# A hybrid decoder layer on one core: split weights of two column blocks kept in DRAM for the second row tile, row sums handed out over more units, first convolution product on ScalarE

## The chip, the cores and the metric

The kernel runs on one core of one Trainium2 chip. The metric is the device time of one execution in microseconds (us); lower is better. A core has a matrix engine (PE, with its weight loads listed as PEld), three engines for elementwise work (VectorE or DVE, ScalarE or ACT, GpSimd or POOL), a queue from which nearly all DMAs are issued (SP), and 16 DMA engines that carry them. Engines run their own instruction lists in a fixed order and wait for each other by semaphores.

## The reference, cut to what matters

One decoder layer on 2048 rows of width 1024. The attention half (two head groups, output projection, LayerNorm) is left as it is by the change. The change lies in the feed-forward half:

```
h = x * (1.0 + scale_f) + shift_f
gate = h @ w_ff_gate                 # 1024 x 2816
up   = h @ w_ff_up                   # 1024 x 2816
gp = jnp.pad(gate, ((0, 0), (CONV_WIDTH - 1, 0), (0, 0)))
conv = sum(gp[:, i:i + S, :] * conv_w[i] for i in range(CONV_WIDTH)) + conv_b   # width 3, along the rows
y = (jax.nn.silu(conv) * up) @ w_down
x = LayerNorm(alpha * x + (1 + gate_f) * y)
```

## The kernel before, in words

**Number format.** Every product is made of float32 operands split into a rounded part and a rest (`hi`, `lo`); three matmuls (hi by hi, hi by lo, lo by hi) stand for one. Splitting one weight part of 128 x 1024 costs a cast on ScalarE (`act.copy`) and a subtraction on VectorE or GpSimd (`tensor_sub`), both in `split`. These go through a helper that raises their priority; all that goes through it carries line 102 in the profile.

**The ring.** Split weights live in a ring of four pairs of tiles `w_hi`, `w_lo` (`ring_pair`). A pair is handed out in the order of the program text and comes free when everything that reads it is done. Raw weights land in `w_raw`, three buffers of 512 KB. In `weights` one part is one DMA into `w_raw`, one cast and one subtraction. For the attention projections `w_in_cols` already keeps the split parts: the first use splits and also stores both halves to DRAM, later uses load the halves into ring pairs.

**Rows and columns of the feed-forward half.** The 2048 rows are four tiles of 512 (0 to 3), taken as two pairs `t2` = 0 and 1. The 2816 columns are 11 blocks `fp` of 256. Most of the gate and up products are done by a seven-product scheme on a pair of row tiles: `unit(n)` is one block, gate or up, for a pair, with products numbered 0 to 6 (lines 1041 to 1043 in `product`). Its weights are made in four ring pieces c, a, b, d by `Weights.make`, and `need` makes pieces three ahead of the product that asks (`WAHEAD = 3`). Pieces c and d are split by ScalarE and VectorE; pieces a and b are sums on VectorE, then cast by ScalarE and subtracted by GpSimd.

**Plain products.** For row pair 0 the first two column blocks (`CL = 2`) are not done by units but by `plain(t, x)`, tile by tile: `plain(0, ...)` while the last tile of the attention half is still being finished, `plain(1, ...)` after the units of pair 0. One call handles two blocks; each block has two weight parts for gate and two for up, so 8 parts a call. Each part feeds 24 matmuls of 128x128 by 128x512 (`col_tile`, lines 293 to 295): 12 for each of the two 128-column halves. Gate sums stand in PSUM tiles `z`, up sums in `wt`, two buffers each.

**Order around the second seam.** Units 0 to 17 are pair 0 (`first` = 18). Unit 17's last call of `need` has by then made pieces c, a and b of unit 18 in the ring, ahead of the parts of `plain(1, ...)` in the program text. Then:

```
run(cols_todo)
spread(sets_of(1, (0, 1, 3, 4, 6)), 5, 5.0, plain(1, [b0[0], tsets[0, 5]]), 10.3 * 2 * CL)
run(sets_of(1, (2, 5)))
```

`sets_of` loads and splits the row operands `t` of pair 1 (DMAs `t<-dh`, `t<-dsum`). Operand sets 2 and 5 of pair 1 take the place of the ones that `plain(1, ...)` reads. `cols_todo` is 26 steps: 18 that transpose and modulate row tiles 2 and 3, then 8 that make sums of their operands on GpSimd (`store_sums`). It is taken three steps at a time after each unit from unit 3 on.

**Convolution.** `conv_silu` is three VectorE operations (lines 1143, 1144, 1145) and one ScalarE activation (line 1146): 40 times on 128x1024 in the units and 8 times on 128x512 in the plain products. Its input `gt` is written by VectorE and ScalarE, its output `cv` has two buffers, freed when their DMAs out (`dsa<-cv`, `da<-cv`) have landed.

Of the kernel before, what the change touches and what calls it, by code (L numbers as in the profile page):

```python
# [20 lines left out]
F32 = mybir.dt.float32  # L21
# [8 lines left out]
P = 128  # L30
# [3 lines left out]
KT = D // P  # L34
# [52 lines left out]
def layer(tc, x, c, w_ada, b_ada, w_in, gla_w_gate, gla_b_gate, sb_norm_g, gla_norm_g, w_out,  # L87
          ln1_g, ln1_b, w_ff_gate, w_ff_up, conv_w, conv_b, w_down, ln2_g, ln2_b, out):
    nc = tc.nc
# [15 lines left out]
    act, dve, pool = Urgent(nc.scalar), Urgent(nc.vector), Urgent(nc.gpsimd)  # L105
# [3 lines left out]
    w_ada, w_in, w_out = w_ada[0], w_in[0], w_out[0]  # L109
    w_ff_gate, w_ff_up, w_down = w_ff_gate[0], w_ff_up[0], w_down[0]  # L110
# [5 lines left out]
    dram = ctx.enter_context(tc.tile_pool(name="dram", bufs=1, space=DRAM))  # L116
# [15 lines left out]
    ccols = const.tile([P, 4 * NFF], F32, name="ccols")  # L132
# [15 lines left out]
    def ring_pair():  # L148

        pool, size = ext.get("pool"), ext.get("size", 0)  # L150
        i = ext.get("i", 0)
        ext["i"] = (i + 1) % (4 + size)
        if i < 4:
            return [wring.tile([P, 1024], F32R, name=f"w_{n}", bufs=4) for n in ("hi", "lo")]
        return [pool.tile([P, 1024], F32R, name=f"w_{n}x", bufs=size) for n in ("hi", "lo")]

    def split(raw, n, nw, lo_eng):
        hi, lo = (w[:, 0:1024 // nw * nw].rearrange("p (k c) -> p k c", c=nw) for w in ring_pair())
        act.copy(hi[:, 0:n], raw[:, 0:n])
        lo_eng.tensor_sub(lo[:, 0:n], raw[:, 0:n], hi[:, 0:n])  # L160
        return hi, lo

    def weights(src, lo_eng, nk=KT, scale=None):

        nw = src.shape[-1]
        per = 1024 // nw
        parts = []
        for k0 in range(0, nk, per):
            n = min(per, nk - k0)
            raw = wring.tile([P, 1024], F32, name="w_raw", bufs=3)  # L170
            raw = raw[:, 0:per * nw].rearrange("p (k c) -> p k c", c=nw)
            nc.sync.dma_start(raw[:, 0:n], src[k0 * P:(k0 + n) * P, :].rearrange("(k p) c -> p k c", p=P))
            if scale is not None:
                pool.tensor_mul(raw[:, 0:n], raw[:, 0:n], scale.unsqueeze(1).to_broadcast([P, n, nw]))
            parts.append(split(raw, n, nw, lo_eng))
        return parts

    dwi = {}

    def w_in_cols(c0, n, k0=0, nk=KT):  # L180

        key = c0, k0
        if key not in dwi:
            parts = weights(w_in[k0 * P:(k0 + nk) * P, c0:c0 + n], pool, nk)
            dwi[key] = []
            per = 1024 // n
            for i, hl in enumerate(parts):
                m = min(per, nk - i * per)
                kept = [dram.tile([P, m, n], F32, name=f"dwi{c0}_{k0}_{i}{j}") for j in "hl"]
                for w, d in zip(hl, kept):  # L190
                    nc.sync.dma_start(d, w[:, 0:m].bitcast(F32))
                dwi[key].append(kept)
            return parts
        parts = []
        for kept in dwi[key]:
            m = kept[0].shape[1]
            hl = [w[:, 0:1024 // n * n].rearrange("p (k c) -> p k c", c=n) for w in ring_pair()]
            for w, d in zip(hl, kept):
                nc.sync.dma_start(w[:, 0:m].bitcast(F32), d)
            parts.append(hl)  # L200
        return parts

    def load_x(t):
        xt = []
        for tb in range(NB):
            xx = pj.tile([P, D], F32, name="t4k", bufs=4)
            nc.sync.dma_start(xx, x[t * TQ + tb * P:t * TQ + (tb + 1) * P, :])
            xt.append(xx)
        return xt

    with tc.tile_pool(name="ada", bufs=1, reuse_waits="tile") as ada:
# [46 lines left out]
        if WLATE:  # L258
            for w, c0 in zip(w_first, (C_SBQ, C_SBK)):
                w += w_in_cols(c0, 256, 4, 4)  # L260
# [28 lines left out]
    def col_tile(ps, w, half, xh, xl, nk=KT, k0=0, k1=None):  # L289
        cs = slice(half * P, (half + 1) * P)  # L290
        for k in range(k0, k1 or nk):
            hi, lo = w[k // 4]
            nc.tensor.matmul(ps, hi[:, k % 4, cs], xh[k], start=(k == 0), stop=False)  # L293
            nc.tensor.matmul(ps, hi[:, k % 4, cs], xl[k], start=False, stop=False)  # L294
            nc.tensor.matmul(ps, lo[:, k % 4, cs], xh[k], start=False, stop=(k == nk - 1))  # L295
# [673 lines left out]
    def direct(i, src):  # L969

        out = []
        for k in range(4):
            w = t_tile(i, k)
            nc.sync.dma_start(w[:, 1, :].bitcast(F32), src[k])
            split_set(w, k)
            out.append(w)
        return out
# [162 lines left out]
    def conv_silu(cv, gt, fb):  # L1140

        n = cv.shape[-1]
        nc.vector.tensor_scalar_mul(cv, gt[:, 0:n], ccols[:, fb:fb + 1])
        nc.vector.scalar_tensor_tensor(cv, gt[:, 1:n + 1], ccols[:, NFF + fb:NFF + fb + 1], cv, ALU.mult, ALU.add)
        nc.vector.scalar_tensor_tensor(cv, gt[:, 2:n + 2], ccols[:, 2 * NFF + fb:2 * NFF + fb + 1], cv, ALU.mult, ALU.add)
        nc.scalar.activation(cv, cv, AF.Silu, bias=ccols[:, 3 * NFF + fb:3 * NFF + fb + 1])

    def plain(t, x):

        xh, xl = ([w[:, i, :] for half in x for w in half] for i in range(2))  # L1150
        for fp in range(CL):
            wg, wu = (weights(w[:, 256 * fp:256 * (fp + 1)], dve) for w in (w_ff_gate, w_ff_up))
            for j in range(2):
                fb = 2 * fp + j
                gp = psm.tile([P, TQ], F32, name="z")
                col_tile(gp, wg, j, xh, xl)
                gt, cv = (x[:, i * (TQ + 2):][:, 0:TQ + 2 - 2 * i] for x in [ft.tile([P, WIDTH["pl"]], F32, name="pl", bufs=2)]
                          for i in range(2))
                nc.gpsimd.tensor_copy(gt[:, 0:2], halo[:, fb, :])
                nc.scalar.copy(gt[:, 2:], gp)  # L1160
                nc.gpsimd.tensor_copy(halo[:, fb, :], gt[:, TQ:])
                conv_silu(cv, gt, fb)
                up = psm.tile([P, TQ], F32, name="wt")
                col_tile(up, wu, j, xh, xl)
                nc.vector.tensor_mul(cv, cv, up)
                nc.sync.dma_start(da[t // 2][:, t % 2 * NB:(t % 2 + 1) * NB, j, fp], cv.rearrange("p (b c) -> p b c", c=P))
                yield 10.3
# [18 lines left out]
    for n in range(first):  # L1186
        unit(n, (0, 2, 1, 3, 4, 5, 6) if n == 0 else range(7),
             {2: lambda: b0.append(direct(2, dh[1][0:4]))} if n + 1 == first else {})
        if n >= 3:
            for _ in range(3):  # L1190
                next(cols_todo, None)
    run(cols_todo)
    spread(sets_of(1, (0, 1, 3, 4, 6)), 5, 5.0, plain(1, [b0[0], tsets[0, 5]]), 10.3 * 2 * CL)
# [105 lines left out]
    for s, (i, b) in enumerate(steps):  # L1299
# [4 lines left out]
        for k in range(NH):  # L1304
            w = wset[i][k]
# [58 lines left out]
```

## Time and profile before

| | us |
|---|---|
| median of 3 runs | 2909.52 |
| lowest, highest | 2899.4, 2913.5 |
| the profiled execution, its own time | 2910.72 |
| its span, first to last instruction | 2909.0 |
| TensorE busy | 2695.8 (93%) |
| VectorE busy | 2092.0 (72%) |
| ScalarE busy | 1126.2 (39%) |
| GpSimd busy | 1206.8 (41%) |
| mean granted TensorE clock | 0.955 of full speed |

The page of the profile gives busy times and the span in 40 slices. The views of the trace used below are tables of stretches (busy time of each engine, granted clock, share of the DMA engines), lists of who waited for whom, groups of instructions by line and shape, and timelines of one engine. In a timeline, a bracket gives the idle time before the instruction and what ended it. A stretch's time is counted from the start of the span. The attention half ends at about 1570 us; units of pair 0 fill the stretch from there to about 1985, `plain(1, ...)` stands between about 1985 and 2047, units of pair 1 follow to about 2480, then comes the down projection.

### The profile page before, as it was taken

Reading aid. Unit: us, or ns where it says so; the run is one execution under the profiler, and the core shown is the slowest. Engines: PE = TensorE matmul, PEld = TensorE weight load, DVE = VectorE, ACT = ScalarE, POOL = GpSimd, SP = SyncE. Lnnn points to the kernel's source line nnn. Section 1 sums busy time; section 2 is a strip of 40 time slices with the busy share of each in tenths; the row PEclk is TensorE's granted clock in tenths of the full one; section 3 lists DMA queues with packets and bytes.
Section 4 is the critical chain, followed back from the end, with each engine's and each line's share of the span. In section 5 each row is a group of like instructions: output and inputs, shape, how many; then the busy total and the mean of one; then the engine's idle time right before and its main releaser. Section 6 shows DMA issues by size and latency. Waiting matters only on the chain. (4 is left out here: it accounts for less than half of the span.)

```text
span 2909.0 us, 38667 instructions
## 1 busy us (share of the span) xinstructions
PE 2695.8 (93%) x13123; PEld 2176.0 (75%) x13123; DVE 2092.0 (72%) x2984; ACT 1126.2 (39%) x1955; POOL 1206.8 (41%) x1271
## 2 busy tenths in 40 slices
PE   7989998989999988989779999898999999999998
PEld 6867887777788765567558778786788888788886
DVE  6375568568878878897676867776777777255988
ACT  2443244365656546534322333223322324332331
POOL 2550222155457674454573455754655554100000
PEclk8989999999999999989789999999999999999999
DMA  8977865767589876466795365545633334655564
GB/s 315 362 251 259 273 237 187 249 193 248 185 261 312 295 245 196 140 200 198 272 335 178 114 182 170 176 133 157 182 110 113 105 106 151 194 169 157 175 211 130
DMA packets 438173, 591.04 MB, mean 203 GB/s; under 512 B 28926, under 2 KB 276952, under 8 KB 437976
## 3 DMA queue, kind: packets, MB, share of 16 engines
q1 hardware_dynamic: 436248, 582.28, 61.9%
q0 software_dynamic: 1728, 6.29, 0.6%
q8 instruction: 104, 1.70, 0.2%
q14 instruction: 93, 0.76, 0.1%
HBM read 417.14 MB, written 171.32 MB: 202 GB/s over the span
## 5 line engine op out<-in xcount | busy, mean ns | idle before, releaser
L563 DVE TENSOR_TENSOR_SCAN pp<-pp,beta 128x512 f32<-128x512 f32 (+2 forms) x320 | 401.5, 1269 | 70.5 <-POOL beta L556 41.7
L565 POOL TENSOR_TENSOR beta<-beta,pp 128x512 f32<-128x512 f32 (+2 forms) x160 | 205.3, 1283 | 291.2 <-DVE pp L563 248.7
L1043 PE MATMUL acc<-t,w_lo 128*128 128x512 f32 x640 | 248.0, 395 | 16.4 <-DVE w_lo L102 16.4
L1041 PE MATMUL acc<-t,w_hi 128*128 128x512 f32 x640 | 252.2, 395 | 4.8 <-ACT k L1099 2.5
L1042 PE MATMUL acc<-t,w_hi 128*128 128x512 f32 x640 | 251.2, 393 | 2.1 <-POOL t L102 2.1
L578 DVE TENSOR_TENSOR wl<-wt,wh 128x512 fp32r<-128x512 f32 (+1 forms) x320 | 185.5, 597 | 71.6 <-ACT wh L577 71.2
L577 ACT CAST wh<-wt 128x512 fp32r<-128x512 f32 (+1 forms) x320 | 161.8, 530 | 180.9 <-PE wt L573 172.9
L551 ACT ACTIVATE pp<-z 128x512 f32<-128x512 f32 (+2 forms) x320 | 173.3, 544 | 138.2 <-PE z L550 83.5
L102 POOL TENSOR_TENSOR w_lo<-wsum,w_hi 128x1024 fp32r<-128x1024 f32 x80 | 204.6, 2558 | 30.4 <-ACT w_hi L102 30.4
L102 ACT CAST w_hi<-w_raw 128x512 fp32r<-128x512 f32 (+2 forms) x169 | 121.4, 740 | 247.5 <-PE acc L1042 93.0
L293 PE MATMUL acc<-hh,w_hi 128*128 128x512 f32 x480 | 194.9, 407 | 3.6 <-DVE st L102 3.0
L573 PE MATMUL wt<-ident,beta 128*128 128x128 f32 x1088 | 184.2, 286 | 14.6 <-DVE beta L565 6.3
L294 PE MATMUL acc<-hl,w_hi 128*128 128x512 f32 x480 | 192.6, 402 | 1.4 <-DVE hl L102 1.4
L295 PE MATMUL acc<-hh,w_lo 128*128 128x512 f32 x480 | 191.4, 400 | 0.5 <-POOL w_lo L102 0.5
L552 ACT ACTIVATE beta<-z 128x512 f32<-128x512 f32 (+2 forms) x320 | 171.2, 543 | 22.6 <-PE wt L573 22.6
L581 PE MATMUL o_ps<-wl,v 128*128 128x512 f32 (+1 forms) x320 | 135.0, 426 | 44.9 <-DVE wl L578 42.5
L573 PEld LDWEIGHTS wt<-ident,beta 128*128 128x128 f32 x1088 | 139.9, 147 | 46.2 <-DVE beta L565 8.8
L1043 PEld LDWEIGHTS acc<-t,w_lo 128*128 128x128 f32 x640 | 121.4, 190 | 45.2 <-DVE w_lo L102 19.8
L549 PE MATMUL z<-k,q 128*128 128x512 f32 (+2 forms) x320 | 140.9, 444 | 13.2 <-ACT beta L552 10.7
L102 ACT CAST w_hi<-wsum 128x1024 fp32r<-128x1024 f32 x80 | 84.0, 1050 | 176.9 <-PE wt L1042 72.8
L102 DVE TENSOR_TENSOR wsum<-w_raw 128x512 f32<-128x512 f32 x80 | 102.8, 1288 | 66.5 <-POOL w_lo L102 54.2
L554 POOL TENSOR_SCALAR_AFFINE_SELECT pp<-pp 128x128 f32<-128x128 f32 x128 | 56.0, 438 | 226.7 <-ACT pp L551 223.1
(341 smaller groups left out, 7603.5 us busy)
## 6 DMA issues: line engine op xcount, KB each, us to landing
w_raw<-in_w_ff_gate_dram SPq DMA_DIRECT2D x48, 512.0 KB
w_raw<-in_w_ff_up_dram SPq DMA_DIRECT2D x48, 512.0 KB
k<-dk SPq DMA_DIRECT2D x160, 128.0 KB
v<-dv SPq DMA_DIRECT2D x80, 256.0 KB
da<-cv SPq DMA_DIRECT2D x40, 512.0 KB
dsa<-cv SPq DMA_DIRECT2D x80, 256.0 KB
w_hi<-dwi_0h SPq DMA_DIRECT2D x39, 512.0 KB
w_lo<-dwi_0l SPq DMA_DIRECT2D x39, 512.0 KB
```

Source lines behind the costliest of these rows:

```text
L102: return f(*args, **kw)
L293: nc.tensor.matmul(ps, hi[:, k % 4, cs], xh[k], start=(k == 0), stop=False)
L294: nc.tensor.matmul(ps, hi[:, k % 4, cs], xl[k], start=False, stop=False)
L295: nc.tensor.matmul(ps, lo[:, k % 4, cs], xh[k], start=False, stop=(k == nk - 1))
L551: nc.scalar.activation(pp[:, 0:n], z[:, 0:n], AF.Sigmoid, scale=-1.0)
L563: nc.vector.tensor_tensor_scan(pp[:, 0:n][:, ::-1], pp[:, 0:n][:, ::-1], beta[:, 0:n], first, ALU.mult, ALU.bypass)
L565: (nc.gpsimd if i in PMU and jt < PMJ else nc.vector).tensor_mul(beta[:, 0:n], beta[:, 0:n], pp[:, 1:n + 1])
L573: pe.transpose(wt[:, i * P:(i + 1) * P], ws[i][:, ks], ident)
L578: nc.vector.tensor_sub(wl[:, cs], wt[:, cs], wh[:, cs])
L1041: nc.tensor.matmul(ps, w[0][:, k, :], t[k][:, 0, :], start=first and k == 0, stop=False, **add)
L1042: nc.tensor.matmul(ps, w[0][:, k, :], t[k][:, 1, :], start=False, stop=False, **add)
L1043: nc.tensor.matmul(ps, w[1][:, k, :], t[k][:, 0, :], start=False, stop=k == 3, **add)
```

## The change

Three edits. First, `w_in_cols`'s keeping of split parts becomes a function `kept_weights(key, src, lo_eng)` that any weights can use, and `plain` uses it: the call for tile 0 splits its 8 parts as before and stores both halves of each to DRAM (16 DMAs of 512 KB), the call for tile 1 loads the halves into ring pairs (16 DMAs of 512 KB) in place of 8 raw loads, 8 casts and 8 subtractions. Second, `cols_todo` is taken two steps at a time from unit 2 on, in place of three from unit 3 on. Third, the first operation of `conv_silu` is `nc.scalar.mul` in place of `nc.vector.tensor_scalar_mul`.

```diff
--- before.py
+++ after.py
@@ -175,30 +175,32 @@
             parts.append(split(raw, n, nw, lo_eng))
         return parts
 
-    dwi = {}
-
-    def w_in_cols(c0, n, k0=0, nk=KT):
-
-        key = c0, k0
-        if key not in dwi:
-            parts = weights(w_in[k0 * P:(k0 + nk) * P, c0:c0 + n], pool, nk)
-            dwi[key] = []
-            per = 1024 // n
+    kept = {}
+
+    def kept_weights(key, src, lo_eng):
+
+        nk, n = src.shape[0] // P, src.shape[1]
+        per = 1024 // n
+        if key not in kept:
+            parts = weights(src, lo_eng, nk)
+            kept[key] = []
             for i, hl in enumerate(parts):
                 m = min(per, nk - i * per)
-                kept = [dram.tile([P, m, n], F32, name=f"dwi{c0}_{k0}_{i}{j}") for j in "hl"]
-                for w, d in zip(hl, kept):
+                kept[key].append([dram.tile([P, m, n], F32, name=f"kept{len(kept)}_{i}{j}") for j in "hl"])
+                for w, d in zip(hl, kept[key][-1]):
                     nc.sync.dma_start(d, w[:, 0:m].bitcast(F32))
-                dwi[key].append(kept)
             return parts
         parts = []
-        for kept in dwi[key]:
-            m = kept[0].shape[1]
-            hl = [w[:, 0:1024 // n * n].rearrange("p (k c) -> p k c", c=n) for w in ring_pair()]
-            for w, d in zip(hl, kept):
+        for pair in kept[key]:
+            m = pair[0].shape[1]
+            hl = [w[:, 0:per * n].rearrange("p (k c) -> p k c", c=n) for w in ring_pair()]
+            for w, d in zip(hl, pair):
                 nc.sync.dma_start(w[:, 0:m].bitcast(F32), d)
             parts.append(hl)
         return parts
+
+    def w_in_cols(c0, n, k0=0, nk=KT):
+        return kept_weights((c0, k0), w_in[k0 * P:(k0 + nk) * P, c0:c0 + n], pool)
 
     def load_x(t):
         xt = []
@@ -1140,7 +1142,7 @@
     def conv_silu(cv, gt, fb):
 
         n = cv.shape[-1]
-        nc.vector.tensor_scalar_mul(cv, gt[:, 0:n], ccols[:, fb:fb + 1])
+        nc.scalar.mul(cv, gt[:, 0:n], ccols[:, fb:fb + 1])
         nc.vector.scalar_tensor_tensor(cv, gt[:, 1:n + 1], ccols[:, NFF + fb:NFF + fb + 1], cv, ALU.mult, ALU.add)
         nc.vector.scalar_tensor_tensor(cv, gt[:, 2:n + 2], ccols[:, 2 * NFF + fb:2 * NFF + fb + 1], cv, ALU.mult, ALU.add)
         nc.scalar.activation(cv, cv, AF.Silu, bias=ccols[:, 3 * NFF + fb:3 * NFF + fb + 1])
@@ -1149,7 +1151,8 @@
 
         xh, xl = ([w[:, i, :] for half in x for w in half] for i in range(2))
         for fp in range(CL):
-            wg, wu = (weights(w[:, 256 * fp:256 * (fp + 1)], dve) for w in (w_ff_gate, w_ff_up))
+            wg, wu = (kept_weights((name, fp), w[:, 256 * fp:256 * (fp + 1)], dve)
+                      for name, w in (("gate", w_ff_gate), ("up", w_ff_up)))
             for j in range(2):
                 fb = 2 * fp + j
                 gp = psm.tile([P, TQ], F32, name="z")
@@ -1186,8 +1189,8 @@
     for n in range(first):
         unit(n, (0, 2, 1, 3, 4, 5, 6) if n == 0 else range(7),
              {2: lambda: b0.append(direct(2, dh[1][0:4]))} if n + 1 == first else {})
-        if n >= 3:
-            for _ in range(3):
+        if n >= 2:
+            for _ in range(2):
                 next(cols_todo, None)
     run(cols_todo)
     spread(sets_of(1, (0, 1, 3, 4, 6)), 5, 5.0, plain(1, [b0[0], tsets[0, 5]]), 10.3 * 2 * CL)
```

## Rows read from the trace of the kernel before

**Rows 1.** The page: busy time, share of the span and instructions of each engine, and the granted TensorE clock in 40 slices of the span, in tenths.

```profile
PE 2695.8 (93%) x13123; PEld 2176.0 (75%) x13123; DVE 2092.0 (72%) x2984; ACT 1126.2 (39%) x1955; POOL 1206.8 (41%) x1271
...
PEclk8989999999999999989789999999999999999999
```

**Rows 2.** Table of four stretches: from and to in us, length, then busy us and number of instructions of PE, PEld, DVE, ACT and POOL, the granted clock, the share of the DMA engines, and GB/s.

```profile
1470.00:1530.00 60.00, 46.77 (x166) 29.60 (x165) 44.80 (x70) 16.61 (x23) 46.59 (x35) 0.83 1.02 367
1600.00:1980.00 380.00, 356.60 (x1552) 289.97 (x1551) 280.63 (x307) 126.77 (x174) 220.16 (x152) 0.97 0.52 159
1980.00:2050.00 70.00, 61.21 (x245) 46.58 (x244) 39.11 (x40) 21.35 (x30) 30.34 (x25) 0.95 0.50 148
2150.00:2450.00 300.00, 300.00 (x1326) 248.39 (x1325) 220.68 (x244) 89.12 (x118) 162.37 (x104) 1.00 0.38 111
```

**Rows 3.** Who PE waited for between 1800 and 2150 us: the waiting PE line, what ended the wait, us in total, times, the longest.

```profile
PE acc L1043 <- DVE w_lo L102: 15.8, 7, 5.1
PE wt L293 <- ACT w_hi L102: 2.8, 3, 1.0
PE wt L1041 <- DVE k L1109: 2.5, 1, 2.5
...
PE z L293 <- ACT w_hi L102: 1.8, 2, 0.9
...
PE z L295 <- DVE w_lo L102: 1.2, 1, 1.2
PE wt L295 <- DVE w_lo L102: 0.6, 1, 0.6
```

**Rows 4.** Groups by line and shape between 1980 and 2050 us: the casts and subtractions of the 8 parts of the plain products of tile 1, with busy us, mean ns, and the idle time of the engine before them and what ended it.

```profile
L102 DVE TENSOR_TENSOR w_lo<-w_raw,w_hi 128x1024 fp32r<-128x1024 f32 x8 | 10.3, 1287 | 18.4 <-ACT w_hi L102 18.4
L102 ACT CAST w_hi<-w_raw 128x1024 fp32r<-128x1024 f32 x8 | 8.4, 1047 | 27.6 <-PE z L294 15.2 <-PE wt L294 10.6 <-DVE pl L1144 1.4
```

**Rows 5.** Timeline of ACT in the same place, two of those casts: start us, length us, the idle time before and what ended it.

```profile
2017.38 1.04 ACT L102 CAST w_hi<-w_raw 128x1024 fp32r<-128x1024 f32 x1 [5.94 <-PE wt L294]
...
2024.40 1.04 ACT L102 CAST w_hi<-w_raw 128x1024 fp32r<-128x1024 f32 x1 [5.97 <-PE z L294]
```

**Rows 6.** Timelines between 1945 and 2100 us, of SP (three loads: start of the issue, its length), then of DVE and ACT (the first instruction that waited for each load's landing).

```profile
2041.92 0.38 SPq L1012 DMA_DIRECT2D w_raw<-in_w_ff_up_dram  x1
...
2044.77 0.32 SPq L974 DMA_DIRECT2D t<-dh  x1
...
2077.69 0.50 SPq L1012 DMA_DIRECT2D w_raw<-in_w_ff_up_dram  x1
...
2046.06 1.29 DVE L102 TENSOR_TENSOR wsum<-w_raw 128x512 f32<-128x512 f32 x2 [0.16 <-DMA w_raw<-in_w_ff_up_dram]
...
2082.82 1.11 DVE L102 TENSOR_TENSOR wsum<-w_raw 128x512 f32<-128x512 f32 x1 [2.30 <-DMA w_raw<-in_w_ff_up_dram]
...
2047.42 0.62 ACT L102 CAST t<-t 128x512 fp32r<-128x512 f32 x1 [0.20 <-DMA t<-dh]
```

**Rows 7.** Table of stretches of 10 us, columns as in rows 2.

```profile
1410.00:1420.00 10.00, 7.59 (x21) 5.03 (x20) 8.60 (x15) 2.84 (x5) 8.57 (x6) 0.51 0.44 160
...
2070.00:2080.00 10.00, 4.92 (x17) 3.71 (x16) 9.90 (x11) 1.57 (x2) 3.79 (x3) 0.76 0.75 213
2080.00:2090.00 10.00, 10.00 (x41) 8.12 (x41) 5.49 (x6) 2.48 (x4) 9.09 (x8) 0.90 0.50 135
2100.00:2110.00 10.00, 10.00 (x45) 8.28 (x45) 6.04 (x4) 2.16 (x3) 9.32 (x5) 1.00 0.46 140
```

**Rows 8.** The first seam: what PE waited longest for between 1380 and 1780 us; timelines of ACT, SP and POOL there; and stretches of 10 us, columns as in rows 2.

```profile
PE acc L791 <- DVE o_in L102: 13.7, 4, 10.7
...
1470.47 1.05 ACT L102 CAST w_hi<-w_raw 128x1024 fp32r<-128x1024 f32 x1 [0.56 <-PE acc L102]
...
1568.47 1.05 ACT L102 CAST w_hi<-w_raw 128x1024 fp32r<-128x1024 f32 x1 [29.34 <-PE acc L443]
...
1513.41 2.31 SPq L789 DMA_DIRECT2D o_in<-do  x3
...
1521.44 5.40 POOL L797 TENSOR_TENSOR o_in<-o_in,o_st 128x512 f32<-128x512 f32 x4 [0.45 <-DMA o_in<-do]
...
1510.00:1520.00 10.00, 2.73 (x4) 1.10 (x4) 4.08 (x5) 2.42 (x4) 8.34 (x6) 0.50 1.06 392
...
1580.00:1590.00 10.00, 10.00 (x45) 8.28 (x45) 10.00 (x23) 2.74 (x6) 1.68 (x2) 1.00 0.52 157
```

**Rows 9.** The convolution's first operation on DVE and its activation on ACT: smallest, median and largest ns of all 40, then the group of line 1143 between 1560 and 2150 us (busy us, mean ns, idle before).

```profile
L1143 DVE TENSOR_SCALAR cv<-gt,ccols x40: 741/751/2958, 1624.8 to 2456.7; 128x1024 f32<-128x1024 f32 x40
...
L1146 ACT ACTIVATE cv<-cv,ccols x40: 1148/1153/1159, 1631.4 to 2466.3; 128x1024 f32<-128x1024 f32 x40
...
L1143 DVE TENSOR_SCALAR cv<-gt,ccols 128x1024 f32<-128x1024 f32 x23 | 33.6, 1463 | 1.6 <-DVE gt L1087 0.6 <-DMA dsa<-cv 0.5 <-issue 0.4
```

**Rows 10.** Timelines of DVE shortly before three of the waits for w_lo in rows 3: the convolution's first operation, and at the last of them the subtractions that PE waited for.

```profile
1827.39 1.98 DVE L1143 TENSOR_SCALAR cv<-gt,ccols 128x1024 f32<-128x1024 f32 x1 [0.53 <-DMA dsa<-cv]
...
1880.89 1.40 DVE L1143 TENSOR_SCALAR cv<-gt,ccols 128x1024 f32<-128x1024 f32 x2
...
2071.49 2.85 DVE L1143 TENSOR_SCALAR cv<-gt,ccols 128x1024 f32<-128x1024 f32 x1
...
2076.66 1.28 DVE L102 TENSOR_TENSOR w_lo<-w_raw,w_hi 128x512 fp32r<-128x512 f32 x2
```


## The prediction

> **What bounds the kernel now.** The page first: TensorE is busy 93% of the span, VectorE 72%, and the granted clock stands near full speed but for a few slices in the middle [rows 1]. Then the table of stretches: between 2150 and 2450 us, units of pair 1, PE is busy all 300 us at clock 1.00, 1326 matmuls, 0.226 us each [rows 2]. Nothing that eases another engine can shorten that stretch. What can be won or lost lies in three places: the first seam (1470 to 1530, where PE has 47 of 60 us and the DMA engines are full), the units of pair 0 (PE 357 of 380), and the second seam (61 of 70) [rows 2]. The list of PE's waits from 1800 to 2150 splits the last two. The units wait for VectorE's subtraction `w_lo`: 15.8 us in 7 waits, the longest 5.1. Line 1109 adds 2.5. The plain products of tile 1 (lines 293 and 295) wait 2.8 + 1.8 + 1.2 + 0.6 = 6.4 us for their casts and subtractions [rows 3]. So VectorE decides in the units, and the making of weights decides a little in the plain products.
>
> **Plain products of tile 1: split weights loaded.** Removed are 8 casts of 1.05 us and 8 subtractions of 1.29 us [rows 4]; ACT and DVE were idle before most of them, so as engine time this gains about nothing. What counts is why they were late: their idle time was ended by PE's own lines 294 of the plain products [rows 4]. Each cast waits until the part before has been read. That is one ring pair in use of four: the text has handed out three pairs to pieces c, a and b of unit 18, which can't all be read until the plain products are done. The casts start 7.0 us apart (2017.4, 2024.4) [rows 5], and 24 matmuls take 5.4 us, so a turn is 5.4 us of matmuls and 1.6 us of refill. The raw part had landed beforehand, in a buffer of its own.
>
> After the change the refill is the DMA. `w_hi` can be issued only when PE has read the last `hi`, `w_lo` only when PE has read the last `lo`, and each load must land before PE goes on. No row shows such a pair waited for in idle. From both sides: a load of 256 KB had its reader start 2.65 us after its issue began (2044.77 to 2047.42); a 512 KB load 4.14 us (2041.92 to 2046.06) and 5.13 us (2077.69 to 2082.82) [rows 6]. The second half of a pair is issued 0.4 us later (length of an issue, rows 6). So a refill is 3.0 to 5.5 us; I take 4.5, because the row with the same size and no wait for its buffer behind it is the 4.14. A turn gets longer by 2.9 us (1.4 to 3.9), eight turns by 23 us (11 to 31). The product of unit 18 that filled a wait before fills one again, so it changes nothing in the difference.
>
> Waits of this length also cost clock. In 2070 to 2090 us PE ran 17 + 41 matmuls where an undisturbed stretch has 45 in 10 us; 32 missing are 7.1 us, and the wait inside was 5.1 [rows 3, 7]. The other 2.0 us is the half clock after it (0.76 and 0.90 granted on average). Of the 8 turns some five end in a wait not filled by other work: 10 us (0 if the clock holds; 43 if all 192 matmuls run at half clock). Together +33 us. SP stands at each load until PE's release; queued behind it are the raw loads of units 18 and 19 and the loads of operand sets 2 and 5, which are needed only after the plain products, so that wait itself costs nothing; if it did, those loads' 4 us would stand in the open.
>
> **Plain products of tile 0: stores added.** Its casts start at 1470 us (first block) and 1568 us (second) [rows 8]. Each block adds 8 stores of 512 KB, 4.2 MB. In the first block's stretch the DMA engines are already full: share 1.02, 367 GB/s [rows 2]. There the last `o_in` loads, issued at 1513.4, were read by GpSimd only at 1521.4, and PE stood 10.7 us for what came of them [rows 8]. What is queued ahead of them on full engines delays them: 4.2 MB at 367 GB/s is +11 us, all on the path (0 if the DMA engines find the time elsewhere). The stores wait on SP for the subtractions, and behind them stand the loads of the output projection's weights, which end in the same wait of PE. The second block's stores meet a share of 0.52 [rows 8] while PE is fully busy: costed at nothing, covered by 10 us of matmuls in every 10; if that cover is gone, up to +5.
>
> **Convolution's first operation on ScalarE.** VectorE loses 40 operations of 128x1024, median 0.75 us but 1.46 us on average between 1560 and 2150 us [rows 9], and 8 small ones. A gate unit has two, so 2.9 us of VectorE. They do lie ahead of the subtractions that PE waited for: 1.98, twice within 1.40, and 2.85 us in the run-up to three of the waits [rows 10]. Of the 15.8 us I take away 10 and of the 2.5 us 1, with 2.0 us of clock for each of two or three long waits: -16 us. Everything gone would be 15.8 + 2.5 + 6 = -24. On ScalarE each costs about 1.15 us, the price of the activation on the same tile [rows 9], about 23 of the 40 before 2150 us; ACT is busy 127 of 380 us there [rows 2], so it hides. Now ACT waits for `gt` and for `cv` to come free (0.53 us of such a wait in rows 10), and casts `w_hi` are queued behind it, for which PE waits at most: up to +5. What is late next is GpSimd's `w_lo` of pieces a and b.
>
> The Trainium skill speaks against this edit: ScalarE: Activation LUTs, section Rules for kernel authors, wants `mul` on VectorE and not on ScalarE. The trace agrees on the single price (1.15 against a median of 0.75 us, rows 9), not that it is VectorE that has the time.
>
> **Sums spread.** 26 steps, two after each unit from unit 2, end with unit 14 in place of unit 11. Nothing is removed; the last sums come three units (84 matmuls each, some 19 us) before the second seam asks for them, which is the cover. 0, or a gain of some 3 us if the bursts on GpSimd and DMA get milder.
>
> **The sum.** 2910.7 (the profiled execution, 1.2 us above the median of the runs) + 33 + 11 - 16 = 2939 us; with the sums' mildness, 2938.
>
> **The rivals.**
> 1. Two ring pairs instead of one (faster). If PE runs products 1 and 3 of unit 18 in the first waits, piece a is read and its pair comes free. Then one part loads (4.5 us) under the 5.4 us of the other, and the 6.4 us of rows 3 vanish in place of +33. 2910.7 - 6 + 11 - 16 = 2899, and 2888 with the stores hidden. It decides as soon as both products can run before the third part. For it: PE has nothing else to do in those waits. Against it: PE waited at part after part [rows 3] without that happening, and product 3 needs a `wt` tile, two of which the plain products hold.
> 2. The lower bounds: refills of 3.0 us, no half clock, stores half hidden. 2910.7 + 11 + 4 - 16 = 2910: the gain and the loss cancel.
> 3. The seam falls to the half clock and stays there. In 1410 to 1420 us PE was busy 7.6 of 10 us at 0.51 granted [rows 7], so busy shares like 5.4 of 9.9 can go with it. 23 + 43 in place of 33: 2972. The Trainium skill has this case in TensorE: Matmul & The Clock Gate, section HAM oscillation: a loop whose matmuls per turn are shorter than its wait for DMA starts each turn at the low clock. Here the matmuls are the longer part, which is why I don't put it first.
> 4. The convolution chain gets longer and decides: each of 40 operations costs 1.15 - 0.75 = 0.4 us more on the path, +16 in place of -16: 2970. Against it: the activation behind it is not what PE waits for in rows 3. This is what the rule of the Trainium skill on `mul` would come to.
>
> **How the numbers follow.** Forecast 0.44 (its own range 2922 to 2960), rival 1 0.19, rival 2 0.21, rival 3 0.12, rival 4 0.04. A measurement of this kernel tells about 0.5% (14.5 us) from no change, so faster means under 2895, slower over 2924. Faster: half of rival 1 and 0.06 of rival 2, 0.16. Same: the rest of rival 1, 0.13 of rival 2 and 0.04 of the forecast, 0.26. Slower: 0.58. The range goes from within rival 1 to rival 3: 2890 to 2975.
>
> **What would show each step.** Right: PE lines 293 and 295 between the seams wait for DMA `w_hi<-kept` and `w_lo<-kept`, 3 to 5 us a time, 25 us or more in all, and the turn grows from 7.0 to about 10 us; PE's wait at line 791 in the first seam grows from 10.7 to about 20 us; waits of line 1043 for VectorE's `w_lo` fall from 15.8 to about 6 us; the stretch of pair 1 stays at PE 300 of 300. Wrong: loads landing within 2 us of the release, DMA share in 1470 to 1530 without longer waits, or waits for `w_lo` that merely move to ACT's casts.

## The result and the profile after

The changed kernel took 2939.96 us (median of 4 runs, 2937.69 to 2947.99) against 2911.51 for the kernel before on the same chip: ratio 1.0104, 95% interval 1.0087 to 1.0122, so slower by some 30 us. The forecast was 2938. The profiled execution took 2937.69 us, its span is 2936.0.

The page of the kernel after: span, busy time of the engines, granted clock in 40 slices [rows 1]. VectorE lost 61 us, ScalarE took 39, PE has the same 13123 matmuls. The slice of the clock that fell from 9 to 7 is the second seam.

```profile
span 2936.0 us, 38675 instructions
PE 2702.3 (92%) x13123; PEld 2184.3 (74%) x13123; DVE 2030.7 (69%) x2928; ACT 1165.6 (40%) x1995; POOL 1206.4 (41%) x1271
...
PEclk9989999999999999989889999997999999999999
```

The table of stretches of the kernel after (columns as in rows 2, which has the same four of before), and the second seam in full length. Pair 1 is still PE 300 of 300. PE's busy time is 5 us less in the first seam's stretch and 17 less in the second's; in the units of pair 0 it is 4 more.

```profile
1470.00:1530.00 60.00, 41.94 (x154) 25.90 (x152) 37.44 (x60) 16.12 (x22) 34.89 (x25) 0.83 1.04 385
1600.00:1980.00 380.00, 360.55 (x1583) 294.76 (x1581) 262.08 (x291) 148.63 (x197) 228.22 (x155) 0.98 0.53 162
1980.00:2050.00 70.00, 44.11 (x146) 33.32 (x144) 23.03 (x21) 7.45 (x12) 22.35 (x19) 0.80 0.44 141
1985.00:2080.00 95.00, 66.36 (x232) 50.67 (x233) 25.00 (x26) 14.35 (x23) 21.62 (x21) 0.84 0.43 140
2150.00:2450.00 300.00, 300.00 (x1325) 248.57 (x1324) 204.76 (x228) 104.73 (x134) 161.66 (x103) 1.00 0.38 112
```

Who PE waited for between 1800 and 2150 us in the kernel after: waiting line, what ended the wait, us, times, longest [rows 3]. Lines have moved by two: 1045 is the old 1043, 295 the old 293 (so too in kernels 4 to 7, 9 and 10 below; kernels 1, 2, 8, 11 and 12 have the lines of before, kernel 3 four more). The waits of 6.4 us for casts and subtractions of the plain products are gone. In their place stand 20.7 us for loads of `w_hi`. The waits for VectorE's `w_lo` are hardly less, 14.9 after 15.8.

```profile
PE acc L1045 <- DVE w_lo L102: 14.9, 5, 4.1
PE z L295 <- DMA w_hi<-kept_1h: 8.7, 2, 5.3
PE acc L1044 <- POOL t L102: 7.2, 2, 6.3
PE z L295 <- DMA w_hi<-kept_0h: 4.4, 1, 4.4
PE wt L295 <- DMA w_hi<-kept_0h: 4.1, 2, 3.4
PE wt L295 <- DMA w_hi<-kept_1h: 3.5, 1, 3.5
```

One turn there, from the timelines of PE and then of SP (start, length, and in brackets the idle time before and what ended it). PE's last matmul of a part starts at 2013.50; SP issues the next `w_hi` at 2013.69; PE goes on at 2017.31. The first matmuls after the wait are 0.43 us apart, the last ones 0.23, and the next wait ends at 2028.18: a turn of 10.9 us, where before had 7.0 [rows 5].

```profile
2013.50 0.39 PE L297 MATMUL z<-t,w_lo 128*128 128x512 f32 x1
2017.31 0.51 PE L295 MATMUL wt<-t,w_hi 128*128 128x512 f32 x1 [3.42 <-DMA w_hi<-kept_0h]
...
2018.46 0.63 PE L296 MATMUL wt<-t,w_hi 128*128 128x512 f32 x1
2018.89 0.63 PE L297 MATMUL wt<-t,w_lo 128*128 128x512 f32 x1
...
2024.07 0.39 PE L296 MATMUL wt<-t,w_hi 128*128 128x512 f32 x1
2024.29 0.39 PE L297 MATMUL wt<-t,w_lo 128*128 128x512 f32 x1
2028.18 0.80 PE L295 MATMUL wt<-t,w_hi 128*128 128x512 f32 x1 [3.50 <-DMA w_hi<-kept_1h]
```

```profile
2013.69 0.33 SPq L198 DMA_DIRECT2D w_hi<-kept_0h  x1
2014.13 0.37 SPq L198 DMA_DIRECT2D w_lo<-kept_0l  x1
2024.49 0.32 SPq L198 DMA_DIRECT2D w_hi<-kept_1h  x1
```

The first seam of the kernel after, PE's waits between 1380 and 1780 us, then SP's issue of `o_in` [rows 8]. The longest wait grew from 10.7 to 14.4 us, and a second one of 4.2 joined it; the loads of `o_in` are issued 9.4 us later (1513.41 before).

```profile
PE acc L793 <- DVE o_in L102: 18.9, 4, 14.4
...
PE acc L776 <- DVE rhl L102: 4.2, 1, 4.2
```

```profile
1522.86 2.88 SPq L791 DMA_DIRECT2D o_in<-do  x4
```

### The profile page after: what moved, and what is told of

It reads as the page before. It is cut to its first block, busy times and chain, and to the rows that moved or that the text cites. A ratio compares the mean times of both kernels' runs of the same rounds, so it can differ in the third digit from the quotient of the medians.

```text
span 2936.0 us, 38675 instructions
## 1 busy us (share of the span) xinstructions
PE 2702.3 (92%) x13123; PEld 2184.3 (74%) x13123; DVE 2030.7 (69%) x2928; ACT 1165.6 (40%) x1995; POOL 1206.4 (41%) x1271
## 5 line engine op out<-in xcount | busy, mean ns | idle before, releaser
L575 PE MATMUL wt<-ident,beta 128*128 128x128 f32 x1088 | 185.0, 288 | 15.8 <-POOL beta L567 5.9
L102 ACT CAST w_hi<-w_raw 128x512 fp32r<-128x512 f32 (+2 forms) x161 | 112.8, 724 | 163.5 <-PE acc L1044 43.1
```

The costliest lines, as they stand in the source:

```text
L102: return f(*args, **kw)
L575: pe.transpose(wt[:, i * P:(i + 1) * P], ws[i][:, ks], ident)
```

## The experiments

Each kernel ran in turn with the kernel before on the same chip. A measured difference in us is the ratio of the two, less 1, times 2911, with its 95% interval in brackets. To see where a kernel gains or loses, the table below takes one instruction that every unit has (VectorE's `k<-k,z`, line 1101 of before) from the timelines and subtracts its start in before: us of delay at units 2 (first seam past), 11, 17 (last of pair 0), 18 and 21 (second seam past) and 39.

```
kernel                          median     ratio 95%       delay at unit 2    11     17     18     21     39
the change                      2939.96  1.0087-1.0122                +3.6   -2.1   +1.4  +26.8  +28.7  +28.2
1 convolution alone             2901.26  0.9948-0.9976                -3.7   -4.6   -9.6   -9.5  -12.8  -13.0
2 sums alone                    2907.70  0.9976-0.9999                -1.7  -10.3   -1.3   -3.5   -3.5   -3.4
3 stores alone                  2915.77  0.9995-1.0025                +8.7   +7.3   +6.7   +6.1   +5.8   +5.9
4 stores and loads              2942.41  1.0080-1.0123                +7.0   +7.3   +8.6  +29.5  +33.7  +33.7
5 convolution and sums          2903.75  0.9956-0.9986                +3.4   -3.0   +1.8   +3.8   +0.4   +0.3
6 the change, four ring pairs   2893.40  0.9922-0.9958                +2.4   -4.8   -2.2   -4.5  -17.4  -17.1
7 number 5, four ring pairs     2894.28  0.9926-0.9959                +4.6   -4.2   -2.1   -0.1  -13.2  -13.4
8 first operation left out      2908.89  0.9980-1.0004                +1.2   +3.6   +4.7   -0.5   -1.9   +2.9
9 the change, two ring pairs    2900.43  0.9953-0.9981                +7.9   +0.8   +5.3   +8.7   -2.7   -1.7
10 the change, three ring pairs 2891.78  0.9921-0.9951                +2.8   -3.9   -0.7   -3.9  -19.9  -18.9
11 before, four ring pairs      2899.14  0.9955-0.9982                +2.4   +0.4   -0.2   -0.9  -14.2  -12.7
12 first operation twice        2926.61  1.0044-1.0077                -6.2   +3.6   +4.7   +8.5   +8.7  +18.8
```

A delay is that of one execution. Kernels 1, 2, 5, 7, 8, 11 and 12 do the same DMA work in the first seam as before, and stand between -6.2 and +4.6 behind it (mean 0.0), so single values mean little under some 5 us. The six kernels with the stores stand between +2.4 and +8.7 (mean 5.4).

**1. The convolution's first operation on ScalarE, alone.**

```
-        nc.vector.tensor_scalar_mul(cv, gt[:, 0:n], ccols[:, fb:fb + 1])
+        nc.scalar.mul(cv, gt[:, 0:n], ccols[:, fb:fb + 1])
```

> The kernel before with one part of the change alone: the convolution's first operation on ScalarE. The forecast's term: -16 us, with PE's waits for VectorE's w_lo between 1800 and 2150 us falling from 15.8 to about 6 us. A second theory, from the changed kernel's trace (where those waits still come to 14.9 us and the units before the second seam gained only some 8 us): VectorE does lose the operation, but its subtraction w_lo starts no earlier, because its queue now waits for ScalarE's result; then -4 to -10 us, and the waits for w_lo stay over 10 us. Rival 4 of the prediction, a longer convolution chain that decides: +5 to +16 us.

Measured: -11 us (-15 to -7). The waits for `w_lo` between 1800 and 2150 us fell to 7.6, but a new one of 5.5 stands at the plain products:

```profile
PE acc L1043 <- DVE w_lo L102: 7.6, 6, 2.5
PE z L295 <- DVE w_lo L102: 5.5, 1, 5.5
```

What follows: smaller than the term, and of the 13 us in this execution's delay only 6 arise in the units of pair 0. Neither account fits whole, and rival 4 has the other sign; kernels 8 and 12 ask whether it is VectorE's time at all.

**2. The sums alone.**

```
-        if n >= 3:
-            for _ in range(3):
+        if n >= 2:
+            for _ in range(2):
```

> The kernel before with the sums alone spread two after each unit from unit 2. The forecast's term: 0, at most -3 us. The rival: it is this edit and not the convolution that gave the changed kernel its some 8 us in the units of pair 0; then -5 to -8 us here and about 0 with the convolution alone.

Measured: -3.5 us (-7 to 0), as the forecast's term had it; the rival fails by kernel 1, where the convolution alone gave 11 and not about 0. The -10 at unit 11 is gone by unit 17 (-1.3); that it is work put off and paid later is argued, from one execution.

**3. The stores alone.** `kept_weights` as in the change, but gate and up are split anew the second time; the convolution and the sums are as before:

```
+        if key in kept and key[0] in ("gate", "up"):
+            return weights(src, lo_eng, nk)
```

> The kernel before with the 16 stores in the plain products of tile 0 alone: the split weights go to DRAM, and tile 1 still loads, casts and subtracts its weights as before. The forecast's term: +11 us, all of it in the first seam, where PE's wait at line 791 grows from 10.7 to over 14 us, and nothing at the second seam. The rival, stores that find idle time on the DMA engines: 0 to +3 us. A third: what the stores cost there is given back before the second seam, so that the seam moves and the end does not; then within 0.1% of the kernel before, with a shift of 7 to 10 us at 1560 us that is gone by 1980 us.

Measured: +2.9 us (-1.5 to +7.3). PE's longest wait at the old line 791 is 14.7 us, much as in the change (14.4), and the delay behind the seam 8.7, of which 3 are given back by the end. The wait, between 1380 and 1780 us:

```profile
PE acc L795 <- DVE o_in L102: 16.8, 2, 14.7
```

The price in the seam is there and stands where the mechanism has it; over the whole run +11 is excluded. Of the two other expectations neither fits whole: the time is that of stores that find idle time, but the wait grew; and the shift isn't gone by 1980 us, 6.7 us of it stand at unit 17.

**4. Stores and loads, without the other two parts.** The change with the convolution and the sums' lines as before.

> The kernel before with stores and loads of the split weights, without the other two parts. If the parts add up, as the forecast has it (+33 and +11): about +36 to +44 us, slower by more than the whole change. If the convolution on ScalarE and the loads get in each other's way at the second seam (the changed kernel has a new wait of 6.3 us there, for an operand of GpSimd's at 1990.8 us), then the loads alone cost less: +25 to +32 us. In either, PE waits for w_hi<-kept five to seven times, 3.4 to 5.4 us each, with turns of 10 to 12 us.

Measured: +29 us (+23 to +36), so nearly all of the change's +30, and under the +36 to +44 of parts that add up. That lies in the second account's range, but doesn't show its reason: the seam (unit 17 to 21) costs 25.1 here and 27.3 in the whole change. PE's wait for GpSimd's operand is here too, shorter (its longest was 6.3 in the change):

```profile
PE acc L1044 <- POOL t L102: 4.4, 2, 3.5
```

**5. Convolution and sums, without the split weights kept.** The change with `weights` in `plain`, as before.

> The changed kernel with the plain products as before, so the convolution on ScalarE and the sums spread and nothing else. Alone these two gave 11 and 3 to 4 us. If both take away the same waits for w_lo, they don't add: -8 to -11 us. If they add: -14 to -15 us, 2897 us. In the changed kernel they gave only some 2 us (the split weights alone cost 30 us, all three parts 28), so a result of -8 us or more here says that the rest was lost where they meet the loads, at the second seam.

Measured: -8.4 us (-12.8 to -4.1), not more than the convolution alone. So the two overlap. 1.0101 x 0.9971 is +21 us for the loads and these two; the change has +30. The difference of 9 is as large as its interval, so whether the rest is lost where they meet the loads stays open. The traces have one place for it, the wait for `POOL t` at the second seam (6.3 us in the change, 3.5 in kernel 4), but by their delays, one execution each, the change stands 5.5 us ahead of kernel 4 at unit 39, where the medians have it 2.5 ahead.

**6. Four ring pairs for the loads.** While a unit ahead of the second seam runs, no piece of a unit behind it is made:

```
-        while made[0] < min(len(todo), place[n, piece] + 1 + WAHEAD):
+        while made[0] < min(len(todo) if n >= first else 4 * first, place[n, piece] + 1 + WAHEAD):
```

> The changed kernel, with the pieces of unit 18 made only after the plain products of tile 1 (while a unit ahead of the second seam runs, nothing of a unit behind it is made). So all four ring pairs are free for the eight loads. The theory of one ring pair, on which the forecast's +33 us rests: the waits for w_hi<-kept and the half clock behind them go, PE's turns fall to about 5.5 us, and the time falls by 20 to 28 us to 2912 to 2920 us, or somewhat less if unit 18 then starts late (a wait of 2 to 6 us for its first pieces). The rival, that the loads themselves are slow (their latency, or the DMA engines busy with other loads): waits of 3 us a part stay, and the time stays within 6 us of the changed kernel's 2940.

Measured: -17.5 us against before (-23 to -12), 46.6 us less than the change, from one line that changes nothing of what is computed. The theory of one ring pair holds, and its price was set too low (2912 to 2920 us were expected): by the delays 42.5 us are gained from unit 17 to 21, the 27.3 that the change had lost there and 15.2 more, for the kernel before pays for its one pair too (kernel 11). No wait for a load is left, the seam runs at clock 0.96, and 378 matmuls fit where the change had 232. Table of stretches and PE's waits between 1985 and 2080 us of this kernel; the one wait left is the late first pieces of the units behind the seam:

```profile
1985.00:2080.00 95.00, 87.83 (x378) 71.47 (x377) 59.42 (x59) 34.63 (x50) 49.12 (x37) 0.96 0.63 199
```

```profile
PE acc L1043 <- ACT w_hi L102: 6.5, 1, 6.5
```

**7. Four ring pairs for the raw weights.** Kernel 5 with the same line.

> The same order of unit 18's pieces, with the plain products' weights loaded raw, cast and subtracted as before, the convolution on ScalarE and the sums spread. By the theory of one ring pair the turn of 7.0 us falls to 5.4 to 5.6 here too, 8 turns x 1.5 us = -8 to -12 us against the same kernel without it (2897 to 2904 us), so 2886 to 2896 us. By the rival, that ScalarE's and VectorE's own queues set the 1.6 us between parts, the time stays.

Measured: 2894 us, 9.5 less than kernel 5, and no wait of the plain products is left, so the rival fails. It equals kernel 6: with the ring free, loading split weights and splitting raw ones cost the same within the runs' scatter.

**8. The first operation left out.** The second one reads `gt` in place of `cv`:

```
-        nc.vector.tensor_scalar_mul(cv, gt[:, 0:n], ccols[:, fb:fb + 1])
-        nc.vector.scalar_tensor_tensor(cv, gt[:, 1:n + 1], ccols[:, NFF + fb:NFF + fb + 1], cv, ALU.mult, ALU.add)
+        nc.vector.scalar_tensor_tensor(cv, gt[:, 1:n + 1], ccols[:, NFF + fb:NFF + fb + 1], gt[:, 0:n], ALU.mult, ALU.add)
```

> The kernel before without the convolution's first operation: it is left out and ScalarE gets nothing in its place (the first tap enters unscaled, so the output differs). This is the most that VectorE's relief alone can give. If VectorE's time is what the units of pair 0 wait for, it gains as much as the forecast's -16 us, up to -24, and more than the 11 us that moving the operation to ScalarE gave; the difference is what ScalarE's longer operation and its wait cost. If it gains no more than 11 us, ScalarE's part was free and the forecast's term was too big because other producers (ScalarE's casts, GpSimd's sums, line 1109) are late next.

Measured: -2.3 us (-6 to +1), less than moving the operation gave, which neither account had. VectorE is busy 17.5 us less in 370 us, and PE 3 us more. The stretch in before and then here:

```profile
1600.00:1970.00 370.00, 348.46 (x1530) 283.87 (x1529) 270.63 (x299) 119.92 (x164) 213.64 (x149) 0.98 0.52 157
```

```profile
1600.00:1970.00 370.00, 351.59 (x1542) 286.44 (x1540) 253.09 (x279) 118.48 (x161) 215.87 (x149) 0.98 0.51 156
```

What PE waited for in its longest wait of this kernel, from the timelines of PE, VectorE and GpSimd. An operation of the convolution that mostly takes 1.28 us takes 3.36 here, beginning 0.52 us after a subtraction of GpSimd's of 2.79 us; the `w_lo` that PE needs stands behind it on VectorE:

```profile
1977.73 0.79 PE L1043 MATMUL acc<-t,w_lo 128*128 128x512 f32 x1 [8.59 <-DVE w_lo L102]
```

```profile
1972.64 3.36 DVE L1144 SCALAR_TENSOR_TENSOR cv<-gt,ccols,cv 128x1024 f32<-128x1024 f32 x1
1975.92 2.36 DVE L102 TENSOR_TENSOR w_lo<-w_raw,w_hi 128x512 fp32r<-128x512 f32 x2
```

```profile
1972.12 2.79 POOL L102 TENSOR_TENSOR w_lo<-wsum,w_hi 128x1024 fp32r<-128x1024 f32 x1
```

**9 and 10. Two and three ring pairs.** Kernel 6 with `4 * first + 2` and `4 * first + 1`: two pieces or one of unit 18 are made ahead.

> The changed kernel with two pieces of unit 18 made ahead of the plain products of tile 1 in place of three, so that two ring pairs serve the eight loads. If what counts is that one part loads under the other's 5.4 us of matmuls, a load of 3.6 to 4.5 us is covered by two pairs, and the time is that of four (2893 us) to within 6 us. If loads are late for another reason (one behind the other on SP, behind the release of the pair), each pair gives about a third of the 46 us between one pair and four: some 2925 us.

> The changed kernel with one piece of unit 18 made ahead, and three ring pairs for the loads. By the first account 2887 to 2896 us: the loads are covered, and unit 18's first piece is ready, so that the wait of 6.5 us that four pairs left in unit 18 (for a cast) gets shorter. By the second some 2909 us.

Measured: 2900.4 and 2891.8 us. From one pair to four the kernel takes 2940, 2900, 2892, 2893: the step is between one and two, where a load first lies under the other part's matmuls. Two pairs came out 7 us above four, one more than the first account allowed, and 25 below the second; three pairs as the first had it. Since kernels 9 and 10 still make pieces of unit 18 ahead, putting off that work isn't what gains. With two pairs waits of 1.2 and 0.9 us are left in 8 turns:

```profile
PE acc L1043 <- ACT w_hi L102: 4.8, 1, 4.8
PE z L295 <- DMA w_hi<-kept_1h: 1.2, 1, 1.2
PE wt L295 <- DMA w_hi<-kept_0h: 0.9, 1, 0.9
```

With three the stretch runs at full clock, 408 matmuls, and no wait over 1.6 us. It is the fastest kernel of all by its median, though kernels 6 and 7 lie within its interval:

```profile
1985.00:2080.00 95.00, 92.74 (x408) 76.18 (x407) 51.96 (x58) 34.78 (x50) 53.61 (x40) 1.00 0.66 214
```

**11. The kernel before with four ring pairs.**

> The kernel before, with nothing of the change in it, and unit 18's pieces made only after the plain products of tile 1. With convolution and sums changed too it ran in 2894 us. If the gain is the ring's alone, 2899 to 2906 us (-6 to -13), and the two other parts give 8 us more, as they did without it; if it needs ScalarE's and VectorE's relief, 2908 to 2914.

Measured: 2899.1 us, -9.3 (-13 to -5), by the delays all of it at the second seam. So the seam's 7.0 us turn was the ring's too, and convolution and sums give some 5 us beside it by the medians (2899 to 2894), 7.6 by the ratios. Unit 18's pieces are late here too; three pairs, which shorten that wait in kernel 10, weren't tried on the kernel before. The wait, between 1985 and 2080 us:

```profile
PE acc L1041 <- ACT w_hi L102: 9.8, 1, 9.8
```

**12. The first operation twice on VectorE.**

> The kernel before with the convolution's first operation issued twice on VectorE (the second writes the same values again). Leaving it out gained 2 to 3 us where the forecast wanted 16. If VectorE's time decided in the units, doubling costs +10 to +16 us. If VectorE mostly shares its time with GpSimd and the waits hang on the order of both, 0 to +5 us, like the leaving out with the sign turned round.

Measured: +17.5 us (+13 to +22), above both accounts' ranges. It would seem to bear out that VectorE's time decides, but the delay says where: +8.7 by unit 21, and 10 more in pair 1, where PE no longer is busy all the time. A stretch there (PE 300 of 300 in rows 2), and PE's waits between 2180 and 2480 us of this kernel:

```profile
2150.00:2450.00 300.00, 295.40 (x1294) 242.00 (x1293) 227.03 (x255) 87.17 (x114) 159.25 (x101) 1.00 0.35 105
```

```profile
PE acc L1043 <- DVE w_lo L102: 4.1, 7, 1.0
```

Work added to VectorE costs there, where taking it away had nothing to gain. About half of this result can therefore not be turned round into a gain for the change.

## Why the prediction came out where it did

**Second seam, forecast +33.** Right in mechanism: one ring pair serves all eight parts, and a load isn't issued before PE has read the one before it (PE's last matmul at 2013.50, the issue at 2013.69; kernels 6, 9, 10). Loads alone cost 29 - 3 = +26 us by the runs, 25 from unit 17 to 21 by the trace. The two halves of the term were both a little large. A refill was put at 4.5 us; PE's waits are 3.4 to 5.3, five of them, and one of 0.7: 20.7 us, less the 6.4 that went, +14 and not +23. The step that failed there is the count: eight turns were charged 2.9 us each, and five paid; for the clock the prediction itself had counted five. Half clock was put at 10: between 1985 and 2080 us 232 matmuls took 66.4 us and need 0.226 each [rows 2], which is 13.9 lost; in before 245 took 61.2 between 1980 and 2050, 5.8 lost: +8. The rest was not in the forecast at all: PE's wait for an operand `t` of GpSimd's at 1990.8 us, 6.3 in place of 2.1. The row of before, then the last load of that operand's set from SP's timeline after:

```profile
PE acc L1042 <- POOL t L102: 2.1, 1, 2.1
```

```profile
1986.36 0.52 SPq L1121 DMA_DIRECT2D da<-cv  x1
1986.97 0.62 SPq L198 DMA_DIRECT2D w_hi<-kept_0h  x1
1987.67 1.03 SPq L198 DMA_DIRECT2D w_lo<-kept_0l  x1
1988.76 0.44 SPq L976 DMA_DIRECT2D t<-dsum  x1
```

It goes out behind a store `da<-cv` that had waited 2.3 us for GpSimd, and behind two loads of `kept` that take 1.7 us to issue; in before all six such loads are issued between 1976.4 and 1983.2. That this order makes the wait is argued, not tried by itself; with two pairs or more the wait is gone.

**First seam, forecast +11, all on the path.** Right place: `o_in` is issued 9.4 us later. The way is argued from SP's waits in the kernel after: between 1480 and 1535 us they come to some 23 us, 20 of them ended by the landing of a transfer, the ones of `o_in` itself among them. The size is wrong: 5.4 us behind the seam (mean of six kernels; 8.7 in kernel 3), +3 (-1.5 to +7.3) at the end. What failed is "all on the path".

**Convolution on ScalarE, forecast -16.** The sign is right, the reason isn't borne out. It stood on VectorE's operations lying ahead of the subtractions that PE waits for [rows 10]; without the operation altogether the gain is 2.3 us. The step that failed is that freed VectorE time shortens the wait in full. Part of the time isn't freed: VectorE's next operation moves up into the same work of GpSimd's and is slowed there. The operation with two inputs that is now the first took 1.89 us on average in kernel 8 between 1600 and 1970 us, and 1.46 in before. Groups there (line, shape, count, busy us, mean ns, idle before): in before the operation that kernel 8 leaves out and the one behind it, then the latter in kernel 8:

```profile
L1143 DVE TENSOR_SCALAR cv<-gt,ccols 128x1024 f32<-128x1024 f32 x18 | 24.5, 1364 | 1.1 <-DMA dsa<-cv 0.5 <-DVE gt L1087 0.4 <-issue 0.2
L1144 DVE SCALAR_TENSOR_TENSOR cv<-gt,ccols,cv 128x1024 f32<-128x1024 f32 x18 | 26.3, 1462 | 0.2
```

```profile
L1143 DVE SCALAR_TENSOR_TENSOR cv<-gt,ccols 128x1024 f32<-128x1024 f32 x18 | 33.9, 1886 | 2.1 <-DMA dsa<-cv 1.7 <-DVE gt L1087 0.4
```

That gives back 7.6 of 24.5 us. Why the 17.5 us by which VectorE is less busy shorten PE's waits so little is shown for the longest wait only. How the slowing comes about shows in all 80 such operations of kernel 8's units: 62 take 1.27 to 1.29 us; the 18 that begin while a two-input operation of GpSimd's runs, or within 0.02 us before it, take 2.0 to 3.5 and end 1.08 us after GpSimd's. In before it is 8 of 80.

The Trainium skill has the mechanism: SBUF — State Buffer, section SBUF: two separate sides, says that VectorE instructions with two SBUF inputs and GpSimd's instructions lock a shared port pair for their whole length, and ScalarE has ports of its own. The trace agrees: 2.27 us from the start of the operation shown for kernel 8 to the end of GpSimd's 2.79, and 1.08, are 3.35 against 3.36 measured; and `nc.scalar.mul` takes 1.13 to 1.16 us in all 40 operations of kernel 1. Why the same operation, moved to ScalarE, gave 8 us more than leaving it out is not settled; the runs' intervals just part (-15 to -7, -6 to +1), and by the delays the two differ by 5 us already behind the first seam. Rival 4 is excluded by kernel 1 (-11 us): its sign is the other one. The Trainium skill's preference for VectorE in a `mul` (ScalarE: Activation LUTs, Rules for kernel authors) would have given that rival; here the measurement decides against it.

**Sums, forecast 0 to -3.** Measured -3.5 us (-7 to 0); nothing failed here.

**The total.** 2938 against 2940 owes something to luck. The parts measured alone make 29 - 11 - 3.5 = +15, the forecast's +28 from 33 + 11 - 16. The seams were too dear by about 15 us. Convolution and sums, added up from kernels 1 and 2, come to nearly the 16 that the convolution was to give alone, but run together (kernel 5) to 8.4. What convolution, sums and loads take from each other, 15 us by the runs with an interval of about 10 either way, made up for the seams. The forecast had no such term, and 9 of the 15 have no cause shown.

**Rivals.** Rival 1 (two ring pairs) was rightly refused, and its price met: it said 2899, and with two pairs given on purpose the kernel takes 2900. There is luck in that too: it holds the same +11 and -16, where the runs have +3 and, with the sums, -8. Rival 2 (2910) fails by its refills of 3.0 us and its unbroken clock: from issue to PE's matmul it was 3.6 us or more, and the clock cost 8 us; its half-hidden stores were right. Rival 3 (half clock throughout) didn't come: 0.84 was granted over the seam. Of the signs named ahead, the length of the waits for `w_hi<-kept`, the turn (10.9 us), and the stretch of pair 1 came out; the waits' sum is 20.7 us and not 25, `w_lo<-kept` never ended a wait of PE's, the wait at the old line 791 reached 14.4 and not 20, and the waits for `w_lo` in the units stayed.

## What to carry to other kernels

Before swapping computed operands for loads, count the buffers that are free at that place: with one, a wait of some 3.5 us a turn and the clock after it were paid here, with two they were nearly gone, and the buffers were held by work made ahead for the next stage. One line that puts that work behind the seam gained 46 us on the change and 9 on the kernel before.

Removing an operation from an engine that another one slows need not give back its time (here 2 us, for 17.5 us less busy), though adding one may cost it; leave it out once, as an experiment, before moving it.

## What the hardware showed beyond expectation

With the DMA engines at a share of 0.43, it takes 3.6 us from the start of the issue of a 512 KB load (`w_hi`, with `w_lo` issued 0.4 us behind it) to PE's first matmul on it (2013.69 to 2017.31, and five more times 3.6 to 4.6); under the same matmuls four pairs load at a share of 0.63 without any wait.

VectorE's operation with two inputs ranges from 1.27 to 3.49 us on the same tile, by whether a two-input operation of GpSimd's is running when it begins: if so, it ends 1.08 us after that one (18 of 80 in kernel 8, 8 in before, 19 in kernel 1). Kernel 8, the convolution's first remaining operation, smallest, median and largest ns of 40:

```profile
L1143 DVE SCALAR_TENSOR_TENSOR cv<-gt,ccols x40: 1269/1279/3487, 1625.3 to 2460.8; 128x1024 f32<-128x1024 f32 x40
```
